# Plain projections for the first pair of width tiles of each SwiGLU, and another pairing of the features in the rest

## The chip, the cores and the metric

The kernel runs on one core of a Trainium2 chip. The metric is the time of one execution in microseconds (us): 1943.27 us, the median of three runs (1942.2 to 1945.07). The engines are named as the profile does: PE is TensorE, DVE is VectorE, ACT is ScalarE, POOL is GpSimd, SP is SyncE, which here only issues transfers. PEld is TensorE's loading of weights beside its matmuls.

## The reference, cut to what matters

A trunk of two layers works on one sequence of 512 tokens with 1024 features, in fp32:

```
D_MODEL = 1024; SEQ = 512; DEPTH = 2; D_FF = 2816
def rms_norm(x, g):
    y = x * rsqrt(mean(x * x, axis=-1, keepdims=True) + 1e-6)
    return y * g
def swiglu(x, w_gate, w_up, w_down):
    return (silu(x @ w_gate) * (x @ w_up)) @ w_down
for layer in range(2):
    x = x + 0.5 * swiglu(rms_norm(x, ffn_pre_norm[layer]), ...)
    x = x + mixer(rms_norm(x, mix_norm[layer]), ...)   # layer 0: even_mixer, layer 1: odd_mixer
    x = x + 0.5 * swiglu(rms_norm(x, ffn_post_norm[layer]), ...)
return rms_norm(x, final_norm)
```

There are four SwiGLUs. The even mixer stands between the first and the second, the odd one between the third and the fourth. The change leaves both mixers' own work as it is.

## The kernel before

x is kept transposed: eight tiles `x[0]` to `x[7]` of 128 features by 512 tokens. PE works on fp32 values split in two, a rounded high part and the rest, so each matrix product is three matmuls: high by high, high by low, low by high (`mm3`, L168 to L170). Weights come in chunks of 128x1024 (512 KB); ACT makes the high part `w_hi` (L120), then DVE the low part `w_lo` (L121).

**A SwiGLU** is `ffn(which, norm, feed)`, which = 0 to 3; the text calls them FFN0 to FFN3. Its width of 2816 is 22 tiles. `Step` s handles the tiles s and s+11 (HF = 11), for gate and up together. The two halves of the features, the two width tiles and the two halves of the tokens (`LO`, `HI`: 256 each) form a two by two block product, done with seven products in place of eight. Each product c is 24 matmuls of 256 columns (L406 to L408) into the banks A, B and D. Products take sums of weight chunks and sums of pieces of x. The seven sums of x are `xt[c, p]`, p = 0 to 3, with feature tile p paired with p+4; `SevenNorm.first`, `diff` and `rest` make them (L264 to L290) as soon as the tiles of x are final. The sums of weights are made by DVE in step 0 (L362) and by accumulating transfers of POOL's queue in the later steps (L351); plain weight loads are issued by SP (L349). The order of the products is `ORDER`, with product 1 of the next step inside. After the steps 3, 7 and 10 comes `down`, the projection back to x (`py`), which ends in DVE's update of `x[d]` (L485).

**The row factor.** RMSNorm's gain is put on x beforehand; its factor per token, `row`, is multiplied in after the products. For it every `x[d]` is squared (`square`: on POOL at L229, the last one on ACT at L227), the squares are added up on POOL (`acc`, L231), PE sums over the partitions (`pc`, L240), DVE makes the root (`rcol`, ten small instructions), PE spreads it (`pr`, L306) and ACT copies it (`R`, L310). `finish_soon(3)` puts `pc` three slots after the beginning of a SwiGLU and `pr` one slot later.

**The order of the work.** Each engine runs its own queue in order. `Stream.run` goes through slots, one product or projection each: first what was put off to this slot (`st.later(n, ...)`), then the splits of weights four items ahead (`split_to`), then loads, then the slot's matmuls. In the slots of a mixer's output projection (`out_proj`) the splits go only to the next slot. A scheduler then moves instructions within each engine's queue, so the queues quoted below are those after it. `feed(d)` is called as soon as `x[d]` is updated: from the last `down` of a SwiGLU (L485, before a mixer or before FFN2), or from `out_proj` (L526, before FFN1 and FFN3). For FFN0 the end of the program text (L1036 to L1071) does it by hand, on x as it arrives.

Of the kernel before, what the change touches and what calls it, by code (L numbers as in the profile page):

```python
# [18 lines left out]
P = 128  # L19
T = 512  # L20
# [12 lines left out]
def trunk_kernel(ctx: ExitStack, tc: tile.TileContext, a, out):  # L33
# [218 lines left out]
    LO, HI = slice(0, 256), slice(256, 512)  # L252

    class SevenNorm(Norm):


        def __init__(self, idx):
            super().__init__(idx)
            self.xt = {}

        def halves(self, c, p, src, g=None):
            t = t2k("r2", f"xt{c}", F32R).rearrange("p (n t) -> p n t", n=2)
            if g is None:
                nc.scalar.activation(t[:, 0], src, AF.Copy)  # L264
                nc.vector.tensor_sub(t[:, 1], src, t[:, 0].bitcast(F32))
            else:
                nc.scalar.activation(t[:, 0], src, AF.Copy, scale=g)
                nc.vector.scalar_tensor_tensor(t[:, 1], src, g, t[:, 0].bitcast(F32),  # L268
                                               op0=OP.mult, op1=OP.subtract)
            self.xt[c, p] = t  # L270

        def first(self, p):
            self.halves(1, p, x[p][:, LO], self.gain(p))

        def diff(self, p):
# [4 lines left out]
        def rest(self, p):  # L280
            q = p + 4
            g, n, nq = self.gain(q), neg_gains[:, self.idx, p:p + 1], neg_gains[:, self.idx, q:q + 1]
            ta, tb = tmp("x37"), tmp("x64")
            b22, x7, x6, x4 = ta[:, LO], ta[:, HI], tb[:, LO], tb[:, HI]
            nc.scalar.activation(b22, x[q][:, HI], AF.Copy, scale=g)
            nc.vector.scalar_tensor_tensor(x7, x[p][:, HI], n, b22, op0=OP.mult, op1=OP.add)
            nc.vector.scalar_tensor_tensor(x6, x[p][:, LO], n, x7, op0=OP.mult, op1=OP.subtract)
# [871 lines left out]
```

## Time and profile before

| what | us |
|---|---|
| median of three runs | 1943.27 |
| the profiled execution: its own time | 1942.9 |
| its span in the trace | 1941.2 |
| PE matmuls, busy | 1834.8 (95%) |
| DVE busy | 1413.3 (73%) |
| ACT busy | 882.4 (45%) |
| POOL busy | 365.3 (19%) |

The span is the time from the first to the last instruction; 1.7 us of the execution's own time lie outside it. A busy share is an average over the whole span: PE has stretches without a gap, hundreds of microseconds long, and a few in which it waits, and its clock is granted in two levels, 1.2 and 2.4 GHz, which the profile writes as shares of the higher one.

### The profile page before, as it was taken

How to read it: one execution, taken by the hardware profiler on the slowest of the kernel's cores; microseconds unless marked ns; L12 is line 12 of the kernel's file. 1: busy time of each engine (PE TensorE's matmuls, PEld its weight loads, DVE VectorE, ACT ScalarE, POOL GpSimd, SP SyncE). 2: the span in 40 equal slices, each digit the busy share in tenths (PEclk: the TensorE clock that was granted, in tenths of full speed). 3: DMA queues.
4: the chain of work that ended last, by engine and by line, in shares of the span. 5: the costliest groups of instructions: out<-in, count | busy, mean ns of one | idle time of the engine just before them, and what ended most of it. 6: DMA issues, size and time to landing. Idle time of an engine off the chain costs nothing.

```text
span 1941.2 us, 29617 instructions
## 1 busy us (share of the span) xinstructions
PE 1834.8 (95%) x11900; PEld 1681.6 (87%) x11900; DVE 1413.3 (73%) x1999; ACT 882.4 (45%) x1319; POOL 365.3 (19%) x310
## 2 busy tenths in 40 slices
PE   4999999989897999999789999999899969999997
PEld 4999989878776989989689898988788769899896
DVE  7866847766759856848987485687798798668474
ACT  5534525433644634525455253444555345345252
POOL 0000000542523000000310000034333230000003
PEclk7999999999997999999999999999999979999999
DMA  4755646412223655655256565542222226556461
GB/s 153 185 152 132 174 119 169 141 59 72 87 87 74 172 148 149 166 127 156 76 142 164 132 178 146 149 133 79 87 88 87 88 62 178 152 142 173 113 166 48
DMA packets 123897, 247.71 MB, mean 128 GB/s; under 512 B 9824, under 2 KB 19952, under 8 KB 123760
## 3 DMA queue, kind: packets, MB, share of 16 engines
q1 hardware_dynamic: 101392, 202.80, 33.2%
q0 software_dynamic: 21792, 41.98, 13.4%
q8 instruction: 93, 1.52, 0.3%
q10 hardware_dynamic: 576, 1.05, 0.1%
q14 instruction: 44, 0.36, 0.1%
HBM read 237.40 MB, written 2.10 MB: 123 GB/s over the span
## 4 chain that ended last, share of the span: by engine, by line
PE 80%; DVE 11%; POOL 4%; ACT 3%; issue 2%; DMA 1%; SPq 0%; DVEq 0%; POOLq 0%; ACTq 0%
PE pA L406 9%; PE py L168 9%; PE py L169 9%; PE pA L407 9%; PE pA L408 9%; PE py L170 8%; PE pD L408 4%; PE pD L407 4%; PE pD L406 4%; PE pB L406 2%; PE pB L407 2%; PE pB L408 2%; DVE w_lo L121 2%; DVE xt L268 1%; POOL q L592 1%
## 5 line engine op out<-in xcount | busy, mean ns | idle before, releaser
L120 ACT ACTIVATE w_hi<-w_raw 128x1024 fp32r<-128x1024 f32 (+1 forms) x455 | 473.7, 1043 | 614.8 <-PE py L169 228.1
L121 DVE TENSOR_TENSOR w_lo<-w_raw,w_hi 128x1024 fp32r<-128x1024 f32 (+1 forms) x455 | 565.1, 1242 | 183.5 <-ACT w_hi L120 151.2
L406 PE MATMUL pA<-xt,w_hi 128*128 128x256 f32 x1408 | 401.5, 285 | 26.1 <-ACT v L418 16.2
L407 PE MATMUL pA<-xt,w_hi 128*128 128x256 f32 x1408 | 400.2, 284 | 0.0
L408 PE MATMUL pA<-xt,w_lo 128*128 128x256 f32 x1408 | 399.9, 284 | 0.0
L351 POOL DMA_DIRECT2D w_raw<-in_gu x80 | 95.3, 1191 | 1075.0 <-DMA w_raw<-in_gu 658.6
L406 PEld LDWEIGHTS pA<-xt,w_hi 128*128 128x128 f32 x1408 | 272.4, 193 | 28.0 <-ACT v L418 18.0
L169 PE MATMUL py<-hl,w_hi 128*128 128x512 f32 x704 | 274.2, 390 | 0.0
L170 PE MATMUL py<-hh,w_lo 128*128 128x512 f32 x704 | 273.9, 389 | 0.0
L168 PE MATMUL py<-hh,w_hi 128*128 128x512 f32 x704 | 273.1, 390 | 0.0
L407 PEld LDWEIGHTS pA<-xt,w_hi 128*128 128x128 f32 x1408 | 272.3, 193 | 0.1
L408 PEld LDWEIGHTS pA<-xt,w_lo 128*128 128x128 f32 x1408 | 271.9, 193 | 0.2 <-DVE w_lo L1057 0.2
L406 PE MATMUL pD<-xt,w_hi 128*128 128x256 f32 x704 | 202.4, 287 | 15.9 <-ACT w_hi L120 15.9
L408 PE MATMUL pD<-xt,w_lo 128*128 128x256 f32 x704 | 202.6, 288 | 7.4 <-DVE w_lo L121 7.4
L407 PE MATMUL pD<-xt,w_hi 128*128 128x256 f32 x704 | 201.9, 287 | 0.0
L485 DVE SCALAR_TENSOR_TENSOR x<-py,x 128x512 f32<-128x512 f32 x96 | 65.9, 688 | 170.6 <-PE py L170 170.6
L168 PEld LDWEIGHTS py<-hh,w_hi 128*128 128x128 f32 x704 | 131.9, 188 | 28.1 <-ACT hh L459 1.2
L169 PEld LDWEIGHTS py<-hl,w_hi 128*128 128x128 f32 x704 | 132.2, 188 | 27.5 <-DVE hl L464 0.8
L170 PEld LDWEIGHTS py<-hh,w_lo 128*128 128x128 f32 x704 | 132.2, 188 | 27.3
L406 PEld LDWEIGHTS pD<-xt,w_hi 128*128 128x128 f32 x704 | 137.9, 196 | 16.8 <-ACT w_hi L120 16.5
L408 PEld LDWEIGHTS pD<-xt,w_lo 128*128 128x128 f32 x704 | 137.9, 196 | 8.0 <-DVE w_lo L121 8.0
L407 PEld LDWEIGHTS pD<-xt,w_hi 128*128 128x128 f32 x704 | 138.0, 196 | 0.3
(218 smaller groups left out, 3330.6 us busy)
## 6 DMA issues: line engine op xcount, KB each, us to landing
w_raw<-in_gu SPq DMA_DIRECT2D x215, 512.0 KB, 4.4
w_raw<-in_gu POOLq DMA_DIRECT2D x80, 512.0 KB, 7.2
w_raw<-in_wd SPq DMA_DIRECT2D x128, 256.0 KB, 2.9
w_raw<-in_wd SPq DMA_DIRECT2D x64, 192.0 KB, 2.5
w_raw<-in_oqk SPq DMA_DIRECT2D x16, 512.0 KB, 3.8
ks<-ks SPq DMA_DIRECT2D x24, 256.0 KB, 3.3
w_raw<-in_eqk SPq DMA_DIRECT2D x8, 512.0 KB, 3.6
w_raw<-in_eo SPq DMA_DIRECT2D x8, 512.0 KB, 4.0
```

What stands on the lines that cost most here:

```text
L120: nc.scalar.activation(hi, raw, AF.Copy)
L121: nc.vector.tensor_sub(lo, raw, hi.bitcast(F32))
L168: nc.tensor.matmul(o, sh, mh, start=first, stop=False)
L169: nc.tensor.matmul(o, sh, ml, start=False, stop=False)
L170: nc.tensor.matmul(o, sl, mh, start=False, stop=last)
L268: nc.vector.scalar_tensor_tensor(t[:, 1], src, g, t[:, 0].bitcast(F32), op0=OP.mult, op1=OP.subtract)
L351: nc.gpsimd.dma_start(t, src, accum_op=OP.add)
L406: nc.tensor.matmul(o, w[0][:, s], t[:, 0], start=new and p + g == 0, stop=False, **go)
L407: nc.tensor.matmul(o, w[0][:, s], t[:, 1], start=False, stop=False, **go)
L408: nc.tensor.matmul(o, w[1][:, s], t[:, 0], start=False, stop=p == 3, **go)
L485: nc.vector.scalar_tensor_tensor(x[d], py[d], 0.5, x[d], op0=OP.mult, op1=OP.add)
L592: nc.gpsimd.tensor_add(q, q, sw)
```

## The change

In every SwiGLU the pair (0, 11) is no longer a step of seven products. It is three slots of ordinary projections over all 512 tokens with x's own high and low parts: `first` (gate and up of tile 0 together, 48 matmuls of 512 columns), `gate` (tile 11, 24 matmuls) and `up` (tile 11, 24). `feed(k)` now splits the whole tile (`split`, L217 and L218), squares it on ACT and adds it on POOL (DVE in FFN0); the sums of x that steps 1 to 10 need are put off by a slot (`sums_for`) or to the end of `up` (`last_sums`). The products 1, 2 and 3 read halves of x's own parts (`whole`). Features are paired anew, with `KLO` and `KHI`; a half of the features is then every other pair of tiles in the chunk, and each weight load of a step, plain or accumulating, is two transfers of 256 KB with rows of 1 KB in place of one of 512 KB with rows of 2 KB. `finish_soon` counts from the first slot: 1 (2 in FFN0) in place of 3. The start of FFN0 is rewritten: x and the first two weight chunks arrive in three cuts, and `sums_for` comes two slots after.

```diff
+    KLO, KHI = (0, 1, 4, 5), (2, 3, 6, 7)
...
+        def halves(self, t, src):
+            nc.scalar.activation(t[:, 0], src, AF.Copy)
+            nc.vector.tensor_sub(t[:, 1], src, t[:, 0].bitcast(F32))
+
+        def whole(self, p):
+
+            k, q = KLO[p], KHI[p]
+            for c, i, s in ((1, k, LO), (2, q, LO), (3, q, HI)):
+                self.xt[c, p] = (self.hi[i][:, s], self.lo[i][:, s])
+
+        def sums_for(self, p):
+            k, q = KLO[p], KHI[p]
+            n, nq = neg_gains[:, self.idx, k:k + 1], neg_gains[:, self.idx, q:q + 1]
+            ta, tb = tmp("x17"), tmp("x26")
+            x1, x7, b22, x6 = ta[:, LO], ta[:, HI], tb[:, LO], tb[:, HI]
+            if p % 2 == 0:
+                self.x4 = tmp("x4")
+            x4 = self.x4[:, (LO, HI)[p % 2]]
+            new = {c: t2k("r2", f"xt{c}", F32R).rearrange("p (n t) -> p n t", n=2) for c in (5, 6, 7)}
+            nc.scalar.activation(b22, x[q][:, HI], AF.Copy, scale=self.gain(q))
+            nc.vector.tensor_sub(x1, x[k][:, HI], x[k][:, LO])
+            nc.vector.scalar_tensor_tensor(x7, x[k][:, HI], n, b22, op0=OP.mult, op1=OP.add)
+            nc.vector.scalar_tensor_tensor(x6, x[k][:, LO], n, x7, op0=OP.mult, op1=OP.subtract)
+            nc.scalar.activation(new[5][:, 0], x1, AF.Copy, scale=n)
+            self.halves(new[6], x6)
+            nc.vector.scalar_tensor_tensor(new[5][:, 1], x1, n, new[5][:, 0].bitcast(F32),
+                                           op0=OP.mult, op1=OP.subtract)
+            self.halves(new[7], x7)
             nc.vector.scalar_tensor_tensor(x4, x[q][:, LO], nq, x6, op0=OP.mult, op1=OP.subtract)
-            self.halves(7, p, x7)
-            self.halves(4, p, x4)
-            self.halves(3, p, b22)
+            for c, t in new.items():
+                self.xt[c, p] = (t[:, 0], t[:, 1])
+            self.rest[p] = x4
+
```

```diff
+        def last_sums(self):
+
+            for p in range(4):
+                k = KLO[p]
+                t = (self.hi[k][:, HI], self.lo[k][:, HI])
+                nc.scalar.activation(t[0], self.rest[p], AF.Copy)
+                nc.vector.tensor_sub(t[1], self.rest[p], t[0].bitcast(F32))
+                self.xt[4, p] = t
+
+        def square(self, k, by_act=False):
+            new = self.acc is None
+            if new:
+                self.acc = t2k("row", "acc")
+            sq = self.acc if new else tmp("sq")
+            nc.scalar.activation(sq, x[k], AF.Square)
+            if not new:
+                (nc.vector if by_act else nc.gpsimd).tensor_add(self.acc, self.acc, sq)
 
         def feed(self, k):
-            if k < 4:
-                self.first(k)
-                self.diff(k)
-            else:
-                self.rest(k - 4)
+            self.split(k)
             self.square(k)
+            if k in KHI:
+                st.later(1, lambda: self.sums_for(KHI.index(k)))
```

```diff
-                            nc.sync.dma_start(t, src)
-                        else:
-                            nc.gpsimd.dma_start(t, src, accum_op=OP.add)
+                        for g in range(2):
+                            src = gu[what[i], g].rearrange("p (a h c) -> p a h c", a=2, h=2)[:, :, what[i + 1]]
+                            dst = t[:, g].rearrange("p (a c) -> p a c", a=2)
+                            if i == 0:
+                                nc.sync.dma_start(dst, src)
+                            else:
+                                nc.gpsimd.dma_start(dst, src, accum_op=OP.add)
                 return go
...
+        def product(f, pg, pu):
+            t = act.tile([P, 2, T], F32, name="gu", tag="e", bufs=3)
+            g, u = t[:, 0], t[:, 1]
+            nc.vector.tensor_mul(g, pg, norm.row)
+            nc.scalar.activation(g, g, AF.Silu)
+            nc.vector.tensor_mul(u, pu, norm.row)
+            nc.vector.tensor_mul(u, u, g)
+            H[f] = split(u, "h", "h")
+
+        banks = {}
+
+        def first(wg, wu):
+            norm.finish_soon(1 + int(which == 0))
+            pg, pu = bank("pg"), bank("pu")
+            for ks in [[k] for k in range(KT)] if which == 0 else (range(KT - 1), range(KT - 1, KT)):
+                for b, w in ((pg, wg), (pu, wu)):
+                    project(b, w, norm, ks)
+            for p in range(4):
+                norm.whole(p)
+            st.later(2 + int(which == 0), lambda: product(0, pg, pu))
+
+        def gate(f):
+            def fn(w):
+                banks[f] = bank("pg")
+                project(banks[f], w, norm)
+            return fn
+
+        def up(f):
+            def fn(w):
+                b = bank("pu")
+                project(b, w, norm)
+                st.later(1, lambda: product(f, banks[f], b))
+                st.later(1, norm.last_sums)
+            return fn
+
+        st.add([chunk(gu[0, 0]), chunk(gu[0, 1])], first, dense=True, raws=6)
+        st.add([chunk(gu[HF, 0])], gate(HF), dense=True, raws=6)
+        st.add([chunk(gu[HF, 1])], up(HF), dense=True, raws=6)
+        add(1, 1)
         for s0, s1 in PARTS:
-            for s in range(s0, s1):
+            for s in range(max(s0, 1), s1):
                 for c in ORDER:
                     if c != 1:
                         add(s, c)
```

```diff
+    raws = [w4("w_raw").rearrange("p n t -> p (n t)") for _ in range(2)]
+    parts = [[w4(n, F32R).rearrange("p n t -> p (n t)") for n in ("w_hi", "w_lo")] for _ in range(2)]
+    cuts = [slice(0, 256), slice(256, 512), slice(512, 1024)]
     for q, s in enumerate(cuts):
-        nc.sync.dma_start(a11[:, :, s], gu0[:, :, s])
-        for k in ((0,), (1,), (2, 3))[q]:
-            load_x(k, LO)
-    st.tokens[0] = lambda: st.slots[0][2].tiles.update(a11=a11)
-    for k in range(4):
-        load_x(k, HI)
-    st.raws = 6
...
-    for k in range(4):
-        first.rest(k)
-        if k == 1:
-            st.split_to(3)
+        ks = ((0, 1), (2, 3), (4, 5, 6, 7))[q]
+        for c in range(2):
+            hi, lo = parts[c]
+            nc.scalar.activation(hi[:, s], raws[c][:, s], AF.Copy)
+            nc.vector.tensor_sub(lo[:, s], raws[c][:, s], hi[:, s].bitcast(F32))
+            for k in (ks[:1], ks[1:])[c]:
+                norms[0].split(k)
+    st.loaded = st.pres = 2
+    st.halves += parts
     for k in range(KT):
-        first.square(k, by_act=True)
+        norms[0].square(k, by_act=True)
+    for p in range(4):
+        st.later(2, lambda p=p: norms[0].sums_for(p))
     st.run()
 
```

The queue of DVE at the end of the even mixer's output projection, before FFN1. Before, `w_lo_5442` and `w_lo_5522` are the weights of that projection's last two slots, `w_lo_5554` those of FFN1's first product, `x3` to `x5` the tiles of x:

```order
L121 TENSOR_TENSOR w_lo_5442<-w_raw_5167,w_hi_5441 128x1024 [waits DMAHW6_49,DMAHW2_49]
L268 SCALAR_TENSOR_TENSOR xt5_5426<-x1_5424,gains_78,xt5_5426 128x256 [waits Activation_49]
L526 TENSOR_TENSOR x4_74<-py_5139,x4_74 128x512 [waits PE_49]
L526 TENSOR_TENSOR x5_75<-py_5152,x5_75 128x512 [waits PE_49]
L286 SCALAR_TENSOR_TENSOR x37_5458<-x0_70,neg_gains_80,x37_5458 128x256 [waits Activation_49]
L121 TENSOR_TENSOR w_lo_5522<-w_raw_5432,w_hi_5521 128x1024 [waits DMAHW7_49]
L287 SCALAR_TENSOR_TENSOR x64_5459<-x0_70,neg_gains_80,x37_5458 128x256 [waits DVE_49]
L121 TENSOR_TENSOR w_lo_5554<-w_raw_5434,w_hi_5553 128x1024 [waits DMAHW0_49,Activation_49]
```

And now, in the same place; `w_lo_5473` is the last slot's, `w_lo_5508` that of FFN1's first projection, and L282 to L264 are `sums_for(1)`:

```order
L264 TENSOR_TENSOR xt7_5401<-x17_5396,xt7_5401 128x256 [waits Activation_49]
L282 TENSOR_TENSOR x17_5413<-x1_71 128x256 [waits Pool_49]
L283 SCALAR_TENSOR_TENSOR x17_5413<-x1_71,neg_gains_80,x26_5414 128x256 [waits Activation_49]
L575 TENSOR_TENSOR x5_75<-py_5118,x5_75 128x512 [waits PE_49]
L284 SCALAR_TENSOR_TENSOR x26_5414<-x1_71,neg_gains_80,x17_5413 128x256 [waits DVE_49]
L287 SCALAR_TENSOR_TENSOR xt5_5415<-x17_5413,neg_gains_80,xt5_5415 128x256 [waits Activation_49]
L290 SCALAR_TENSOR_TENSOR x4_5398<-x3_73,neg_gains_80,x26_5414 128x256 [waits DVE_49]
L264 TENSOR_TENSOR xt6_5416<-x26_5414,xt6_5416 128x256 [waits Activation_49]
L264 TENSOR_TENSOR xt7_5417<-x17_5413,xt7_5417 128x256 [waits Activation_49]
L121 TENSOR_TENSOR w_lo_5473<-w_raw_5382,w_hi_5472 128x1024 [waits DMAHW7_49]
L218 SCALAR_TENSOR_TENSOR xl_5443<-x4_74,gains_78,xh_5442 128x512 [waits Activation_49]
L121 TENSOR_TENSOR w_lo_5508<-w_raw_5384,w_hi_5507 128x1024 [waits DMAHW0_49,PE_49,Activation_49]
```

The sums of x for two pairs (L282 to L264, one set of seven stands here, the other lies just before) are now ahead of the last slot's weights, where parts of `first` and `diff` and one instruction of `rest` were.

PE's queue near the beginning of FFN2. Before, the row sums `pc` stood between the product 5 (into D) and the product 2 (into B):

```order
L407 MATMUL pD_9220<-xt5_8977,w_hi_9082 128x256
L408 MATMUL pD_9220<-xt5_8977,w_lo_9083 128x256
L240 MATMUL pc_9273<-ones1_87,acc_8884 128x1 [waits Pool_49]
L240 MATMUL pc_9273<-ones1_87,acc_8884 128x1 x3
L406 MATMUL pB_9305<-xt2_9017,w_hi_9179 128x256 [waits Activation_49]
L407 MATMUL pB_9305<-xt2_9017,w_hi_9179 128x256
L408 MATMUL pB_9305<-xt2_9017,w_lo_9180 128x256 [waits DVE_49]
```

And now, between `first` (into `pg` and `pu`) and `gate`:

```order
L168 MATMUL pu_9113<-xh_9082,w_hi_9002 128x512
L169 MATMUL pu_9113<-xl_9083,w_hi_9002 128x512
L170 MATMUL pu_9113<-xh_9082,w_lo_9003 128x512
L240 MATMUL pc_9162<-ones1_87,acc_8810 128x1 [waits Pool_49]
L240 MATMUL pc_9162<-ones1_87,acc_8810 128x1 x3
L168 MATMUL pg_9196<-xh_8806,w_hi_9055 128x512
L169 MATMUL pg_9196<-xl_8807,w_hi_9055 128x512
L170 MATMUL pg_9196<-xh_8806,w_lo_9056 128x512
```

The row sums have moved from 48 matmuls of 256 columns behind the beginning of the SwiGLU to 48 of 512 columns, and the last matmuls ahead of them are those that read `x7`'s parts.

DVE's queue at the beginning of FFN0. Before, with the sums of weights (L362) and of x (L286, L287):

```order
L362 TENSOR_TENSOR w_sum_112<-w_raw_108,w_raw_110 128x1024 [waits DMAHW4_49,DMAHW3_49]
L362 TENSOR_TENSOR w_raw_108<-w_raw_108,w_raw_96 128x1024 [waits DVE_49]
L121 TENSOR_TENSOR w_lo_159<-w_sum_112,w_hi_158 128x1024 [waits Activation_49]
L286 SCALAR_TENSOR_TENSOR x37_162<-x0_70,neg_gains_80,x37_162 128x256
L362 TENSOR_TENSOR w_sum_112<-w_sum_112,w_raw_96 128x1024 [waits DVE_49]
L287 SCALAR_TENSOR_TENSOR x64_163<-x0_70,neg_gains_80,x37_162 128x256 [waits DVE_49]
```

And now; `acc` is the sum of squares, `w_lo_186` belongs to `gate`, `w_lo_192` to `up`, and L191 and L194 are the first of the ten small instructions of `rcol`:

```order
L218 SCALAR_TENSOR_TENSOR xl_157<-x7_77,gains_78,xh_156 128x512 [waits DMAHW5_49,Activation_49]
L311 TENSOR_TENSOR acc_160<-acc_160,sq_180 128x512 [waits DVE_49]
L121 TENSOR_TENSOR w_lo_186<-w_raw_183,w_hi_185 128x1024 [waits DMAHW6_49,Activation_49]
L282 TENSOR_TENSOR x17_267<-x0_70 128x256
L283 SCALAR_TENSOR_TENSOR x17_267<-x0_70,neg_gains_80,x26_268 128x256 [waits Activation_49]
L191 TENSOR_SCALAR rs0_378<-pc_372 128x4 [waits PE_49]
L284 SCALAR_TENSOR_TENSOR x26_268<-x0_70,neg_gains_80,x17_267 128x256 [waits DVE_49]
L287 SCALAR_TENSOR_TENSOR xt5_270<-x17_267,neg_gains_80,xt5_270 128x256 [waits Activation_49]
L290 SCALAR_TENSOR_TENSOR x4_269<-x2_72,neg_gains_80,x26_268 128x256 [waits DVE_49]
L264 TENSOR_TENSOR xt6_271<-x26_268,xt6_271 128x256 [waits Activation_49]
L264 TENSOR_TENSOR xt7_272<-x17_267,xt7_272 128x256 [waits Activation_49]
L282 TENSOR_TENSOR x17_284<-x1_71 128x256
```

The ten small instructions now stand among `sums_for`'s.

## Rows read from the trace of the kernel before

**Rows 1.** The page: busy us of the engines, share of the span, instructions.

```profile
PE 1834.8 (95%) x11900; PEld 1681.6 (87%) x11900; DVE 1413.3 (73%) x1999; ACT 882.4 (45%) x1319; POOL 365.3 (19%) x310
```

**Rows 2.** Windows: stretch, length, busy us (count) of PE, PEld, DVE, ACT, POOL; clock; DMA share; GB/s.

```profile
117.69:161.24 43.55, 43.55 (x194) 36.06 (x193) 20.75 (x23) 11.35 (x12) 3.58 (x3) 1.00 0.51 122
190.03:230.35 40.32, 40.32 (x338) 40.32 (x337) 34.23 (x38) 22.81 (x28) 3.57 (x3) 1.00 0.66 171
```

**Rows 3.** Windows: the starts of the SwiGLUs, to the end of step 0's third product.

```profile
0.00:57.21 57.21, 30.00 (x204) 29.23 (x205) 44.94 (x88) 32.70 (x61) 5.14 (x12) 0.82 0.54 157
569.61:635.08 65.47, 49.42 (x290) 44.69 (x289) 58.94 (x86) 30.71 (x53) 21.88 (x16) 0.84 0.32 81
953.97:996.59 42.62, 27.16 (x206) 26.55 (x205) 37.02 (x63) 21.47 (x39) 11.22 (x8) 0.84 0.38 99
1541.60:1607.93 66.33, 49.12 (x289) 44.29 (x287) 59.69 (x87) 30.63 (x53) 22.65 (x17) 0.82 0.30 80
```

**Rows 4.** Waits of PE: line waited for, total us, times, longest us.

```profile
PE pA L406 <- ACT v L418: 16.2, 2, 15.4
PE pD L406 <- ACT w_hi L120: 15.9, 3, 7.4
PE py L170 <- DVE w_lo L121: 15.3, 2, 8.2
PE pc L240 <- POOL acc L231: 11.3, 1, 11.3
```

**Rows 5.** Timeline of PE: matmuls at the start of FFN1 (start us, duration, operation).

```profile
585.89 0.80 PE L170 MATMUL py<-mh,w_lo 128*128 128x512 f32 x1 [7.07 <-DVE w_lo L121]
...
589.47 0.63 PE L169 MATMUL py<-m,w_hi 128*128 128x512 f32 x1
```

**Rows 6.** Timeline of DVE at the start of FFN1.

```profile
572.03 1.29 DVE L526 TENSOR_TENSOR x<-py,x 128x512 f32<-128x512 f32 x2 [0.82 <-PE py L170]
573.30 0.82 DVE L268 SCALAR_TENSOR_TENSOR xt<-x,gains,xt 128x256 fp32r<-128x256 f32 x1
574.05 2.70 DVE L277 TENSOR_TENSOR x<-x 128x256 f32<-128x256 f32 x2
...
581.63 0.48 DVE L268 SCALAR_TENSOR_TENSOR xt<-x,gains,xt 128x256 fp32r<-128x256 f32 x1
...
593.85 0.41 DVE L265 TENSOR_TENSOR xt<-x,xt 128x256 fp32r<-128x256 f32 x1
```

**Rows 7.** Timeline of POOL in the same place, and at the start of FFN2.

```profile
572.81 1.04 POOL L229 TENSOR_TENSOR acc<-x 128x512 f32<-128x512 f32 x1 [10.81 <-DVE x L526]
573.81 1.22 POOL L229 TENSOR_TENSOR sq<-x 128x512 f32<-128x512 f32 x1
575.11 1.36 POOL L231 TENSOR_TENSOR acc<-acc,sq 128x512 f32<-128x512 f32 x1
...
971.80 2.98 POOL L231 TENSOR_TENSOR acc<-acc,sq 128x512 f32<-128x512 f32 x1 [4.66 <-ACT sq L227]
```

**Rows 8.** DMA issues: KB each, median us from issue to landing.

```profile
w_raw<-in_gu SPq DMA_DIRECT2D x215, 512.0 KB, 4.4
w_raw<-in_gu POOLq DMA_DIRECT2D x80, 512.0 KB, 7.2
w_raw<-in_wd SPq DMA_DIRECT2D x128, 256.0 KB, 2.9
```

**Rows 9.** Timeline: one accumulating load, the split that reads it, and the product after.

```profile
191.48 1.19 POOL L351 DMA_DIRECT2D w_raw<-in_gu  x1 [9.47 <-DVE gu L435]
...
201.68 1.06 ACT L120 ACTIVATE w_hi<-w_raw 128x1024 fp32r<-128x1024 f32 x1 [1.02 <-PE pD L407]
...
210.19 0.28 PE L406 MATMUL pA<-xt,w_hi 128*128 128x256 f32 x1
```

**Rows 10.** Timeline of ACT and DVE at FFN0's beginning.

```profile
14.03 0.51 ACT L285 ACTIVATE x<-x,gains 128x256 f32<-128x256 f32 x1 [2.31 <-DMA x<-in_xT]
...
15.82 1.22 DVE L121 TENSOR_TENSOR w_lo<-w_sum,w_hi 128x1024 fp32r<-128x1024 f32 x1
```

More of the change, by code (lines that the diff above doesn't have):

```diff
@@ L295, in feed @@
-        def feed(self, k):
-            if k < 4:
-                self.first(k)
-                self.diff(k)
-            else:
-                self.rest(k - 4)
+            self.xt, self.rest = {}, {}
+        def halves(self, t, src):
[5 more added lines that the diff above has]
+                self.xt[c, p] = (self.hi[i][:, s], self.lo[i][:, s])
@@ L346, in go @@
                     for i in range(0, len(what), 2):
-                        src = gu[what[i]].rearrange("g p c -> p g c")[:, :, what[i + 1] * T:(what[i + 1] + 1) * T]
-                        if i == 0:
-                            nc.sync.dma_start(t, src)
-                        else:
-                            nc.gpsimd.dma_start(t, src, accum_op=OP.add)
+                        for g in range(2):
[5 more added lines that the diff above has]
+                                nc.gpsimd.dma_start(dst, src, accum_op=OP.add)
                 return go
@@ L365, in new @@
                     r["z"] = w4("w_sum")
-                if self.s > 0:
+                if True:
                     by_sum = {
@@ L405, in fn @@
                             s = slice((g * 4 + p) * P, (g * 4 + p + 1) * P)
-                            nc.tensor.matmul(o, w[0][:, s], t[:, 0], start=new and p + g == 0, stop=False, **go)
-                            nc.tensor.matmul(o, w[0][:, s], t[:, 1], start=False, stop=False, **go)
-                            nc.tensor.matmul(o, w[1][:, s], t[:, 0], start=False, stop=p == 3, **go)
+                            nc.tensor.matmul(o, w[0][:, s], t[0], start=new and p + g == 0, stop=False, **go)
+                            nc.tensor.matmul(o, w[0][:, s], t[1], start=False, stop=False, **go)
+                            nc.tensor.matmul(o, w[1][:, s], t[0], start=False, stop=p == 3, **go)
                     for n, aux in enumerate(after):
@@ L493, in add @@
             st.add([steps[s].item(c)], steps[s].slot(c), dense=True, raws=6)
-        add(0, 1)
-        first, end, fn, dense, raws = st.slots[-1]
-        def begin(w):
-            norm.finish_soon(3)
-            fn(w)
-        begin.tiles = steps[0].raw
-        st.slots[-1] = (first, end, begin, dense, raws)
+        def product(f, pg, pu):
[32 more added lines that the diff above has]
+        add(1, 1)
         for s0, s1 in PARTS:
-            for s in range(s0, s1):
+            for s in range(max(s0, 1), s1):
                 for c in ORDER:
@@ L1033, in trunk_kernel @@
     ffn(3, norms[5], last_feed)
[L1036 to L1068 removed]
+    raws = [w4("w_raw").rearrange("p n t -> p (n t)") for _ in range(2)]
+    parts = [[w4(n, F32R).rearrange("p n t -> p (n t)") for n in ("w_hi", "w_lo")] for _ in range(2)]
+    cuts = [slice(0, 256), slice(256, 512), slice(512, 1024)]
+    for q, s in enumerate(cuts):
+        for c in range(2):
+            nc.sync.dma_start(raws[c][:, s], a["gu0"][0, c][:, s])
+            if q == 0:
+                nc.sync.dma_start(x[c], a["xT"][c])
+        for k in ((), (2, 3), (4, 5, 6, 7))[q]:
+            nc.sync.dma_start(x[k], a["xT"][k])
+    for q, s in enumerate(cuts):
+        ks = ((0, 1), (2, 3), (4, 5, 6, 7))[q]
+        for c in range(2):
+            hi, lo = parts[c]
[5 more added lines that the diff above has]
+    st.halves += parts
     for k in range(KT):
[L1070 removed]
+        norms[0].square(k, by_act=True)
+    for p in range(4):
+        st.later(2, lambda p=p: norms[0].sums_for(p))
     st.run()
```

45 lines of the change are left out of this document (removed).

## The prediction

> **What bounds the kernel now.** I read the page first: PE is busy for 95% of the span [rows 1], so only two things can move the time much, PE's own work and the few places where it stands. Then the windows over a stretch without gaps. A projection runs 192 matmuls of 512 columns in 43.55 us, 0.227 each; two steps of seven products run 336 matmuls of 256 columns in 40.32 us, 0.120 each, so a product takes 2.88 us and a step 20.16 [rows 2]. In both PE is busy throughout at the full clock, and DVE has time left. Third, the same view over the four starts, each up to the end of the third product of step 0, which is where step 1's product 5 begins: 57.21, 65.47, 42.62 and 66.33 us long, with PE idle for 27.2, 16.1, 15.5 and 17.2, together 76, and a clock of 0.82 to 0.84 [rows 3]. The list of waits names what ends last there: the x sums and weight sums that the first products need (one `pA` wait of 15.4, `pD` waits up to 7.4), the weights of the output projection (8.2), the sum of squares (11.3) [rows 4]. The steady part is bound by PE alone; the starts are bound by DVE's queue and what it shares with POOL.
>
> **Work of PE.** Up to the mark there are eight products before, 192 x 0.120 = 23.0 us. Now there are 96 matmuls of 512 columns and product 1 of step 1: 96 x 0.227 + 2.9 = 24.7. That is 1.6 us more per SwiGLU, 6.5 in all, and it is contained in the four sums below.
>
> **FFN0.** Before, the mark is at 57.21 [rows 3]. x4 was in by 14.03, behind 2.75 MB with it [rows 10]; all of x and two weight chunks are 3 MB, so x7 is in by about 15 and its parts are ready at 16.5. The low part of `gate`'s weights follows on DVE at about 18, which is also when `first` ends. From there PE has 5.4 + 0.8 + 5.4 of work, to about 30. The row factor decides: its ten small instructions stand among `sums_for`'s. DVE has four sets of sums, each seven operations of 0.41 to 0.48 us that overlap by 0.07, 2.6 a set [rows 6], so 10.5; three weight splits of 1.22, overlapping likewise, 3.4 [rows 10]; leftover additions of squares and the ten small ones, some 3; and waits for ACT, some 1.5. That is 36.4. Then `pr`, 0.4, and product 1, 2.9 at the full and 5.8 at the half clock: about 42.5, a gain of 14.7. Bounds: if the scheduler's order keeps the factor off the lane, PE's own work ends about 36 at the low clock (gain 21); if every sum waits for ACT, about 48 (gain 9).
>
> **FFN1 and FFN3.** What PE needs next is `w_lo_5473`, now queued behind two sets of sums. From 572.03 [rows 6] DVE has six updates of x at 0.64, 3.9; four low parts of x at about 0.70 (between 0.48 for 256 columns and 1.22 for 1024, [rows 6, 10]), 2.8; `w_lo_5393`, 1.1; two sets of sums, 5.2; its own 1.1. Together 14.1, so 586.1 undisturbed. POOL holds DVE up: between 573.30 and 576.75 three operations that take 0.48 + 0.41 + 0.41 alone took 0.82 + 2.70 [rows 6], 2.2 more, while POOL was at work for nearly all of that time [rows 7]; the updates, which read PSUM, kept their 0.64. Weighted by the kind of operation I take 0.6 of POOL's time. Five additions of 1.36 fall there: 4.1. The low part is done at 590.2, PE goes on at 590.5. It was ready for it at about 584: before, it ended its earlier matmuls 7.07 us before 585.89 [rows 5], and the chunk that it waited for then is now split early, so it has 22 matmuls more first. So 6.5 us of waiting; before, matmuls behind such a wait were 0.63 long at an interval of 0.43 instead of 0.227 for ten of them, from 585.89 past 589.47 [rows 5], so 2.0 for the clock. Then 20 matmuls of the projection, 4.5; the ordinary pair, 21.8; `pc` and `pr`, 1.2; product 1, 2.9. The mark falls at 590.5 + 2.0 + 4.5 + 21.8 + 1.2 + 2.9 = 622.9 instead of 635.08, a gain of 12.2. FFN3 has the same queues and nearly the same window: 12.2 again. What hides the rest: `first` reads x7's parts only in its last six matmuls, 9.5 us behind its beginning, and the sums of squares are wanted 10.9 behind it. Bounds: undisturbed (no loss beside POOL) the gain is 16.3, without a clock loss 18.9; with the sums of the next pairs in front of the following weights too, 5.
>
> **FFN2.** PE comes from the last `down` without a gap and has 953.97 as its beginning [rows 3]. Before, it stood 11.3 us for the last addition of squares [rows 4], done at 974.78 [rows 7], and at 0.8 and 3.4 for others. Now POOL has seven additions instead of seven products and seven additions, and DVE no weight sums. The last update of x can be made at 954; square, two additions and a split later is about 959, and `pc` is due at 953.97 + 10.9 = 964.9: covered by six microseconds. The mark: 953.97 + 10.9 + 0.8 + 5.4 + 0.4 + 5.4 + 2.9 = 979.8, and 1 us for the row factor's ten small steps, which `gate`'s 5.4 only just covers: 980.8 instead of 996.59, a gain of 15.8. Bounds 12 to 16.8.
>
> **The steady part.** The products of steps 1 to 10 are the same matmuls. Their loads are doubled in number. SP issues ten instead of five per step; POOL four instead of two, 1.19 each [rows 9], 4.8 us in a step of 20.16, so neither queue is full. The later half of an accumulating load is issued 1.2 later. Its cover: issued at 191.48, landed 7.2 later [rows 8], the split begins at 201.68 and PE needs it at 210.19 [rows 9]; with 1.06 and 1.22 for the two splits some 9 us of delay cost nothing, 8 with what else stands in those queues. Nearest rows: 256 KB loads take 2.9 where 512 KB take 4.4 [rows 8], so two in a row 1.3 times as long; twice as long would be 14.4, a delay of 7.2. Both are under the cover. I take 0 for the 40 steps, with 0 to 10 as bounds; no gain, since nothing is waited for there.
>
> **The sum.** 14.7 + 12.2 + 15.8 + 12.2 = 54.9. The profiled execution took 1942.9 us, 1.7 beside its span: 1888.0. The median of the three runs is 0.4 above it, so 1888.4; I say 1888.
>
> **The rivals.**
> Lost again at the starts: DVE becomes the bound of every start, since splits of x, sums and weight splits are on one lane. For it: DVE is busy for 58.9 of 65.5 us there already [rows 3], and its queue has the sums ahead of weights. Against it: the weight sums (four of 1.22) go, and so do four low parts per pair. Priced by the lower bounds, 9 + 6 + 12 + 6 = 33 are gained: 1910.
> Held for the whole: DVE loses the full time of each addition on POOL. For it: where DVE's operations read SBUF alone, it lost 2.2 us beside about 3 of POOL's [rows 6, 7], more than the 0.6 that I take as the mean. Against it: the updates of x between them lost nothing. 5 x 1.36 = 6.8 instead of 4.1 in FFN1 and FFN3, 2.7 later at each: 1893. The Trainium skill, "SBUF — State Buffer", section "Who interferes with whom", says this of a DVE instruction with two SBUF inputs and a GpSimd instruction that reads SBUF: one excludes the other for the whole instruction. By that rule the time would be that of this rival; the rows agree in kind, and lie between it and the forecast in size.
> More than forecast: POOL and DVE get out of each other's way, because half of POOL's work went to ACT, and the row factor of FFN0 is not held up. For it: ACT is busy less than half of each start [rows 3]. Against it: the additions on POOL remain. 18 + 17.5 + 16.8 + 17.5 = 70: 1873.
> Slower than before: the smaller transfers with 1 KB rows fall behind. Place: the accumulating loads of steps 1 to 10. It decides from a landing more than 15.5 us after the issue, against 7.2 now: each microsecond beyond is lost 40 times, and from 1.4 us per step the gain is eaten. At 2 per step, 80 - 55 = 25 worse: 1968. For it: the DMA engines are busy for 0.66 of a steady stretch [rows 2], and the loads come in turn. Against it: the landing would have to double and more. The Trainium skill, "DMA: Bandwidth & Descriptors", section "Rules for kernel authors", asks to coalesce transfers into large ones, which speaks for this rival; no row here shows accumulating loads of the smaller form.
> The starts stay as they are: the waits are only renamed, with another lane as slow. Against it: the 11.3 us for the squares and the 15.4 of FFN0 have known causes in work that goes. 1943.
>
> **How the numbers follow.** Forecast 50%, held for the whole 13%, more than forecast 15%, lost again at the starts 15%, transfers 5%, no difference 2%. The time is the likeliest's, 1888. The range takes the forecast with the bounds of its four terms (about 1877 to 1903), the greater gain down to 1868, and the case of 1910 with 12 us beyond, to 1922; what lies outside are the transfers, the unchanged start and the tails. A measurement of this kernel can tell 0.2%, some 4 us, from no change. Faster 0.93, same 0.02, slower 0.05.
>
> **What would show it.** Marks at about 42.5, 608, 954 and 1553 (the later ones shifted by the gains before them); `pc` of FFN2 without a wait; one wait of about 6 us of PE for a low part of weights in each output projection before FFN1 and FFN3; a wait of some 7 us for the row factor in FFN0; 40.32 us for two steps as before; accumulating loads that land in 8 to 14 us. Wrong would be: gaps of PE inside steps 1 to 10, waits for `w_hi` behind a DMA there, a wait for `acc` in FFN2, or a start that is no shorter.

## The result, and the profile after

The changed kernel takes 1889.67 us, the median of four runs (1887.48 to 1890.68), against 1943.24 of the kernel before beside it: a ratio of 0.9722, with a 95% interval of 0.9705 to 0.9739. Run a second time beside the last experiments it took 1887.32 (0.9703, 0.9689 to 0.9718), so a difference of 2 to 3 us between two kernels below is not told from none. 1888 was predicted, in a range of 1868 to 1922.

The first row of the page, as in [rows 1]: PE is busy for the same 1835 us; what went is idle time, 52 us of the span.

```profile
PE 1834.6 (97%) x11612; PEld 1663.2 (88%) x11612; DVE 1359.1 (72%) x1949; ACT 875.4 (46%) x1302; POOL 415.0 (22%) x369
```

The windows, columns as in [rows 2]: the four starts up to step 1's product 5, which answer to [rows 3], and two steps of seven products, which answer to the second of [rows 2].

```profile
0.00:43.53 43.53, 31.56 (x133) 25.73 (x133) 36.70 (x79) 28.21 (x52) 8.71 (x15) 0.88 0.80 218
555.75:610.12 54.37, 49.01 (x219) 39.91 (x218) 46.36 (x77) 32.09 (x53) 17.39 (x13) 0.91 0.42 97
928.98:955.17 26.19, 26.19 (x133) 22.09 (x132) 24.63 (x45) 13.61 (x24) 7.04 (x6) 1.00 0.49 114
1500.64:1555.78 55.14, 48.51 (x217) 39.09 (x215) 47.11 (x78) 32.02 (x53) 17.49 (x13) 0.94 0.41 96
176.57:216.89 40.32, 40.32 (x339) 40.32 (x338) 34.24 (x38) 22.82 (x28) 6.49 (x6) 1.00 0.70 175
```

The halves of the accumulating loads, which answer to the second row of [rows 8]:

```profile
w_raw<-in_gu POOLq DMA_DIRECT2D x160, 256.0 KB, 5.3
```

The starts are shorter by 13.7, 11.1, 16.4 and 11.2 us, 52.4 together, which is the whole difference of the spans (1941.2 and 1888.9). PE's idle time in them fell from 76 to 24 us. Its busy time in them stayed (155.3 against 155.7), though the prediction reckons with 6.5 us more work: less of it ran at the low clock (a clock of 0.88 to 1.00 instead of 0.82 to 0.84). FFN2's start has no gap any more and runs at the full clock. The steady steps take the same 40.32. PE's waits, as in [rows 4]:

```profile
PE pg L168 <- ACT w_hi L120: 10.0, 2, 5.1
...
PE pr L322 <- DVE rcol L202: 6.3, 1, 6.3
PE pg L168 <- ACT xh L217: 5.5, 1, 5.5
...
PE py L170 <- DVE w_lo L121: 2.0, 3, 0.8
```

The waits of [rows 4] for sums and for `acc` are gone. What is left at the starts are one wait of some 5 us in each output projection with short ones for low parts of weights behind it, FFN0's wait for the row factor, and its first 5.5 us, until the first high part of x is made. The matmuls at FFN1's beginning (start, duration, operation, wait before it), as in [rows 5]:

```profile
575.52 0.80 PE L168 MATMUL pg<-xh,w_hi 128*128 128x512 f32 x1 [4.86 <-ACT w_hi L120]
576.82 0.79 PE L170 MATMUL py<-mh,w_lo 128*128 128x512 f32 x1 [0.50 <-DVE w_lo L121]
```

And DVE's queue there, as in [rows 6], then POOL's, as in [rows 7]:

```profile
558.17 1.89 DVE L575 TENSOR_TENSOR x<-py,x 128x512 f32<-128x512 f32 x3 [0.82 <-PE py L170]
...
562.04 2.33 DVE L121 TENSOR_TENSOR w_lo<-w_raw,w_hi 128x1024 fp32r<-128x1024 f32 x1
564.29 1.78 DVE L218 SCALAR_TENSOR_TENSOR xl<-x,gains,xh 128x512 fp32r<-128x512 f32 x1
565.99 1.51 DVE L282 TENSOR_TENSOR x<-x 128x256 f32<-128x256 f32 x1
...
571.67 0.68 DVE L575 TENSOR_TENSOR x<-py,x 128x512 f32<-128x512 f32 x1
572.27 0.89 DVE L284 SCALAR_TENSOR_TENSOR x<-x,neg_gains,x 128x256 f32<-128x256 f32 x1
573.08 0.47 DVE L287 SCALAR_TENSOR_TENSOR xt<-x,neg_gains,xt 128x256 fp32r<-128x256 f32 x1
573.48 1.48 DVE L290 SCALAR_TENSOR_TENSOR x<-x,neg_gains,x 128x256 f32<-128x256 f32 x1
...
575.55 1.21 DVE L121 TENSOR_TENSOR w_lo<-w_raw,w_hi 128x1024 fp32r<-128x1024 f32 x1
```

```profile
561.81 5.41 POOL L311 TENSOR_TENSOR acc<-acc,sq 128x512 f32<-128x512 f32 x3 [13.93 <-ACT sq L309]
571.38 1.50 POOL L311 TENSOR_TENSOR acc<-acc,sq 128x512 f32<-128x512 f32 x1 [4.15 <-ACT sq L309]
573.21 1.47 POOL L311 TENSOR_TENSOR acc<-acc,sq 128x512 f32<-128x512 f32 x1 [0.34 <-ACT sq L309]
...
583.62 1.29 POOL L311 TENSOR_TENSOR acc<-acc,sq 128x512 f32<-128x512 f32 x1 [6.83 <-ACT sq L309]
```

The three operations that meet the first three additions are each 1.0 to 1.1 us longer than alone (1.21, 0.74, 0.41); those additions take 1.8 each, where one that met none of them, at 583.62, takes 1.29. The update at 571.67, which reads PSUM, runs beside an addition at its usual 0.68.

### The profile page after: what moved, and what is told of

It is laid out like the page before. It is cut to its first block, busy times and chain, and to the rows that moved or that the text cites. A ratio compares the mean times of both kernels' runs of the same rounds, so it can differ in the third digit from the quotient of the medians.

```text
span 1888.9 us, 29622 instructions
## 1 busy us (share of the span) xinstructions
PE 1834.6 (97%) x11612; PEld 1663.2 (88%) x11612; DVE 1359.1 (72%) x1949; ACT 875.4 (46%) x1302; POOL 415.0 (22%) x369
## 3 DMA queue, kind: packets, MB, share of 16 engines
q0 software_dynamic: 43552, 41.98, 15.1%
## 4 chain that ended last, share of the span: by engine, by line
PE 82%; DVE 7%; POOL 4%; ACT 3%; issue 2%; DMA 1%; SPq 0%; DVEq 0%; POOLq 0%; ACTq 0%
PE py L168 10%; PE py L170 10%; PE py L169 9%; PE pA L424 8%; PE pA L425 8%; PE pA L426 8%; PE pD L426 4%; PE pD L425 4%; PE pD L424 4%; PE pB L426 2%; PE pB L425 2%; PE pB L424 2%; POOL q L641 1%; DVE w_lo L121 1%; ACT e L690 1%
## 5 line engine op out<-in xcount | busy, mean ns | idle before, releaser
L424 PE MATMUL pA<-xh,w_hi 128*128 128x256 f32 x640 | 182.7, 285 | 0.0
L425 PE MATMUL pA<-xl,w_hi 128*128 128x256 f32 x640 | 182.1, 285 | 0.0
L426 PE MATMUL pA<-xh,w_lo 128*128 128x256 f32 x640 | 182.1, 285 | 0.0
L424 PE MATMUL pA<-xt,w_hi 128*128 128x256 f32 x640 | 181.2, 283 | 0.0
L426 PE MATMUL pA<-xt,w_lo 128*128 128x256 f32 x640 | 181.1, 283 | 0.0
L425 PE MATMUL pA<-xt,w_hi 128*128 128x256 f32 x640 | 181.1, 283 | 0.0
L424 PEld LDWEIGHTS pA<-xh,w_hi 128*128 128x128 f32 x640 | 123.9, 194 | 1.5 <-ACT v L436 1.4
L425 PEld LDWEIGHTS pA<-xl,w_hi 128*128 128x128 f32 x640 | 123.9, 194 | 0.1
L426 PEld LDWEIGHTS pA<-xh,w_lo 128*128 128x128 f32 x640 | 123.9, 194 | 0.0
L424 PEld LDWEIGHTS pA<-xt,w_hi 128*128 128x128 f32 x640 | 122.9, 192 | 0.2 <-ACT v L436 0.2
L426 PEld LDWEIGHTS pA<-xt,w_lo 128*128 128x128 f32 x640 | 122.9, 192 | 0.0
L425 PEld LDWEIGHTS pA<-xt,w_hi 128*128 128x128 f32 x640 | 122.9, 192 | 0.0
```

The lines of the kernel that those rows point to most:

```text
L424: nc.tensor.matmul(o, w[0][:, s], t[0], start=new and p + g == 0, stop=False, **go)
L425: nc.tensor.matmul(o, w[0][:, s], t[1], start=False, stop=False, **go)
L426: nc.tensor.matmul(o, w[1][:, s], t[0], start=False, stop=p == 3, **go)
```

## The experiments

Times are medians; "the changed kernel" is 1887 to 1890. Edits are against the changed kernel where nothing else is said. The ratios are to the kernel before, which took 1944.4, 1943.8 and 1945.4 beside the three groups of experiments. "Marks" below are the beginnings of step 1's product 2 in a SwiGLU (in the kernel before, of step 0's), and a stretch goes from one mark to the next.

**Squares on POOL again.**

```diff
-            nc.scalar.activation(sq, x[k], AF.Square)
+            if by_act or k == KT - 1:
+                nc.scalar.activation(sq, x[k], AF.Square)
+            else:
+                nc.gpsimd.tensor_mul(sq, x[k], x[k])
```

> The changed kernel with the squares of x's tiles 0 to 6 made on POOL again (the change's other parts stay). Theory (DVE's queue, held up beside POOL, sets the starts): in each of FFN1 and FFN3 five multiplies of some 1.2 us come to stand beside DVE's sums, of which DVE loses 0.65, so the low part of the last slot's weights comes 3.9 us later in each; FFN2 hides it or loses up to 3. 8 to 11 us slower than the changed kernel, 1898 to 1901. Rival (the squares on ScalarE are where most of the gain comes from): over 25 us slower, above 1915. Second rival (POOL does not hold up DVE): 1890.

Measured 1906.48, 0.9802 (0.9788 to 0.9817): 17 to 19 slower, between the theory's range and the rival's. FFN1 and FFN3 lost 3 to 5 each by their marks, as the theory had it. Nearly half of the loss lies where the theory allowed 0 to 3, in FFN2. Its window, 26.19 long in the changed kernel, and the waits of PE:

```profile
930.99:966.00 35.01, 30.55 (x133) 24.31 (x133) 32.00 (x51) 16.14 (x27) 11.76 (x9) 0.90 0.42 94
```

```profile
PE pg L168 <- ACT w_hi L120: 15.7, 2, 8.0
...
PE pg L169 <- DVE xl L218: 3.2, 2, 2.2
```

The first row of waits belongs to the output projections (10.0 in the changed kernel), the second to FFN2. There PE is idle for 4.5 us, 3.2 of it for x's low parts, which stand on DVE between operations held up, and part of the window runs at the low clock (0.90). So the squares' place does matter where DVE is just able to keep up.

**The kernel before with its squares on ACT** (against before; 0, 2, 3 and 5 are the four SwiGLUs' norms).

```diff
-            if by_act or k == KT - 1:
+            if by_act or k == KT - 1 or self.idx in (0, 2, 3, 5):
```

> The kernel before with all squares of the four SwiGLUs made on ACT, and nothing else of the change. Putting them back on POOL cost the changed kernel 17 us. Theory (the squares hold DVE's queue up in either kernel, by what stands there): FFN1 and FFN3 gain 3 to 5 each, FFN2's wait of 11.3 for the sum of squares shrinks by 3 to 8: 1924 to 1935. Rival (the squares matter only where the sums of x are delayed as in the changed kernel): 1939 to 1945. Second rival (they were the main cost of the starts): below 1915.

1923.91, 0.9894 (0.988 to 0.9909): 20 faster than before, at the theory's better end. FFN1, FFN2 and FFN3 gained 6 to 6.5 each by their marks, for FFN1 and FFN3 more than the theory's 3 to 5. PE's waits for the low parts of the output projection's weights fell from the 15.3 of [rows 4] to 3.8: with the squares off POOL, DVE makes those parts sooner. The sum of squares is still waited for, though for 8.5 instead of 11.3, and the long waits for sums are untouched:

```profile
PE pA L406 <- ACT v L418: 16.2, 2, 15.4
PE pD L406 <- ACT w_hi L120: 16.1, 3, 8.2
...
PE pc L240 <- POOL acc L231: 8.5, 1, 8.5
...
PE py L170 <- DVE w_lo L121: 3.8, 2, 2.4
```

So the squares are worth 17 to 20 of the 54 us by either kernel. The other 34 to 37 are a difference and no run has them alone: they hold the ordinary pair, the new pairing and FFN0's rewritten start, whose window alone is 13.7 shorter.

**Sums of x at once.**

```diff
-                st.later(1, lambda: self.sums_for(KHI.index(k)))
+                self.sums_for(KHI.index(k))
```

> The changed kernel with the sums of x of FFN1, FFN2 and FFN3 made as soon as the tiles are final, and not a slot later, so only the ordinary first pair, the pairing and the squares on ACT are left of the change there. Theory (what the ordinary pair gives is time: nothing of the sums is needed until 22 us after its beginning, so their exact place matters only where weights or x's parts wait behind them): FFN2 0 to 2 slower, FFN1 and FFN3 2 to 6 slower each, 1892 to 1904. Rival (the delay by a slot is what pays): over 1910.

1890.9, 0.9723 (0.9709 to 0.9738): the same as the changed kernel, just under the theory's range. The delay by one slot is worth nothing that can be measured. By elimination, what pays is that nothing needs the sums for the length of the ordinary pair; no run tests that alone.

**Half loads in the kernel before.**

```diff
-                        if i == 0:
-                            nc.sync.dma_start(t, src)
-                        else:
-                            nc.gpsimd.dma_start(t, src, accum_op=OP.add)
+                        for q in range(2):
+                            cut = slice(q * 256, (q + 1) * 256)
+                            if i == 0:
+                                nc.sync.dma_start(t[:, :, cut], src[:, :, cut])
+                            else:
+                                nc.gpsimd.dma_start(t[:, :, cut], src[:, :, cut], accum_op=OP.add)
```

> The kernel before, with each weight load of its steps as two transfers of 256 KB with rows of 1 KB, plain and accumulating, and nothing else of the change. Theory (nothing waits for these loads in the steps, and they have 8 us in hand): no difference, 1941 to 1946. Rival (smaller transfers cost time that the change then had to make up for): 2 us per step or more, above 1990; or, if halves land sooner, faster at the starts, by up to 5.

1945.36, 1.0006 (0.9996 to 1.0016): no difference. Two steps still take 40.32 us, and the accumulating halves land in a median of 5.7 us after their issue, where whole loads took 7.2 [rows 8]:

```profile
191.59:231.91 40.32, 40.32 (x339) 40.32 (x338) 34.24 (x38) 22.84 (x28) 7.25 (x6) 1.00 0.70 171
```

```profile
w_raw<-in_gu POOLq DMA_DIRECT2D x160, 256.0 KB, 5.7
```

**Additions of squares on DVE in FFN1 and FFN3.**

```diff
-            self.square(k)
+            self.square(k, by_act=self.idx in (2, 5))
```

> The changed kernel with the additions of squares of FFN1 and FFN3 on DVE instead of POOL. Theory (POOL's additions hold DVE up: in the changed kernel DVE's operations in front of the last slot's weights took 4.4 us more than the same operations alone): with none of them DVE does the five additions in 3.0 and nothing is held, so the weights come 1.4 earlier in each, 1886 to 1889. Rival (the longer operations have another cause, such as ACT's or a DMA's use of the same memory): DVE's operations stay as long, and the additions come on top, 3 us later in each, 1895 to 1898.

1883.74, 0.9683 (0.9667 to 0.9699): 4 to 6 faster by the medians, more than the theory said, though the interval overlaps that of the changed kernel's second run. By the marks FFN3's stretch is 3.6 shorter and FFN1's 1 to 3. The rival is out by the trace: with no addition on POOL there, the operations that took 2.33, 1.78 and 1.51 in the changed kernel take what they take alone, beside the same squares on ACT:

```profile
563.29 0.74 DVE L218 SCALAR_TENSOR_TENSOR xl<-x,gains,xh 128x512 fp32r<-128x512 f32 x1
...
564.55 1.21 DVE L121 TENSOR_TENSOR w_lo<-w_raw,w_hi 128x1024 fp32r<-128x1024 f32 x1
565.69 0.41 DVE L282 TENSOR_TENSOR x<-x 128x256 f32<-128x256 f32 x1
```

**The row factor first in FFN0.**

```diff
-            norm.finish_soon(1 + int(which == 0))
+            norm.finish_soon(1)
...
-        st.later(2, lambda p=p: norms[0].sums_for(p))
+        st.later(3, lambda p=p: norms[0].sums_for(p))
```

> The changed kernel, with FFN0's sums of x put off by one more slot and its row factor asked for one slot earlier, so that the ten small instructions stand at the head of DVE's queue behind the split of gate's weights. Theory (DVE's order sets FFN0's beginning: PE waited 6.3 us for the row factor and then ran product 1 at half the clock, 2.6 more): the wait for the factor falls to 2 at most, and then the weights' low part for product 1 is late, by about 4; the mark at 43.5 moves to 38 to 40, 1884 to 1887. Rival (the lane is full whatever its order): 43.5 stays, 1890.

1886.71, 0.9701 (0.9687 to 0.9716). The trace shows the theory's order of things: the wait of 6.3 for the factor is gone, product 1 waits 1.2 and product 5 0.75 for weights,

```profile
32.69 0.39 PE L424 MATMUL pA<-xh,w_hi 128*128 128x256 f32 x1 [1.21 <-ACT w_hi L120]
33.94 0.39 PE L424 MATMUL pD<-xt,w_hi 128*128 128x256 f32 x1 [0.75 <-ACT w_hi L120]
```

and product 2 of step 1 begins at 43.9 instead of 49.5 (48.2 in the changed kernel's second run). Not all of that is kept: at 45.8 PE waits 1.46 for the high part of the next product's weights, a wait that the changed kernel does not have there. The time alone, 1 to 3 us better than the changed kernel's two medians, does not tell it from no change.

**Sums behind the projection's weights in FFN1 and FFN3.**

```diff
-            if k in KHI:
+            if k in KHI and self.idx == 3:
                 st.later(1, lambda: self.sums_for(KHI.index(k)))
...
             for p in range(4):
                 norm.whole(p)
+            if which in (1, 3):
+                for p in range(4):
+                    st.later(1, lambda p=p: norm.sums_for(p))
```

> The changed kernel with all sums of x in FFN1 and FFN3 put off until the first slot of the ordinary pair has begun, so that they stand behind the weights of the output projection in DVE's and ACT's queues. Theory (PE's two waits in each output projection, 5.4 and 6.6 us together, and the half clock after them, some 3, come from the sums that stand in front of weights; the ordinary pair has room for 10.5 us of sums): both waits go, 8 us in each, 1872 to 1876. Rival (the sums are then late for product 5 of step 1, and the time is only moved): 1886 to 1892.

1886.04, 0.9695 (0.968 to 0.9709): at the better edge of the rival's range. In FFN1 the wait for weights fell, from 5.4 to 2.1, and did not go as the theory had it; 2.7 came back as a wait for the row factor, whose ten instructions now stood behind the sums:

```profile
571.73 0.66 PE L170 MATMUL py<-mh,w_lo 128*128 128x512 f32 x1 [2.09 <-DVE w_lo L121]
...
598.54 0.65 PE L322 MATMUL pr<-ident,rcol 128*128 128x128 f32 x4 [2.65 <-DVE rcol L202]
```

FFN1's stretch is as long as in the changed kernel. FFN3's is 3.4 shorter; there the wait for the factor is 1.2. So the rival holds for FFN1 and only in part for FFN3.

**Both, with the sums one slot later still** (`st.later(2, ...)` in the last edit, and the edit for FFN0).

> The changed kernel with FFN0's order as in the run with the row factor first, and with the sums of x in FFN1 and FFN3 behind the projection's weights and behind the row factor's instructions. Theory (the run with the sums late took away most of PE's wait for weights, but put the sums in front of the row factor, which gave 4 us back in FFN1 and 2 to 3 in FFN3): FFN0 gains 5, FFN1 3 to 6, FFN3 4 to 7 against the changed kernel: 1873 to 1880. Rival (DVE is full between the last update of x and product 5, so a wait comes up at product 1 or 5 in place of the factor's): 1881 to 1886.

1880.57, 0.967 (0.9655 to 0.9685), at the border of the two ranges. FFN0 and FFN3 gained 5 and 4 by their marks, FFN1's stretch nothing: there the scheduler filled DVE with three sets of sums before the factor, which PE then awaited for 3.9.

**Row factor first, additions on DVE** (the two edits together).

> The changed kernel with the row factor first in FFN0 and the additions of squares of FFN1 and FFN3 on DVE. Theory (the two gains lie in different starts and add up: 5.4 in FFN0, 2.8 and 3.6 in FFN1 and FFN3 by the marks of the two single runs): 11 to 12 us faster than the changed kernel, 1877 to 1880 by the medians. Rival (what one gains at a start is taken back in the next): 1883 or more.

1881.3, 0.967 (0.9654 to 0.9686), 6.0 better than the changed kernel beside it: neither range. FFN1's stretch, from FFN0's mark to its own, took 566.8 us here and 563.5 in the run with the additions alone. Of the 3.3 us between them, 1.5 is the wait that the row factor's new place brings right behind FFN0's mark. It stands in all four runs with the factor first and in none of the others:

```profile
46.07 0.39 PE L424 MATMUL pA<-xt,w_hi 128*128 128x256 f32 x1 [1.46 <-ACT w_hi L120]
```

So the rival is right for that part: of what FFN0 gains by its mark, 1.5 is given back in the next product. The other 1.8 is no more than what the two runs of the changed kernel differ by in the same stretch (566.4 and 564.7), and its cause is open.

**All three, the last two sets of sums later still** (`st.later(2 if p < 2 else 3, ...)`).

> As the run before, and the sums of x in FFN1 and FFN3 put behind the weights of the projection, the last two sets behind the row factor's instructions. Theory: with nothing held up and no sums in front of weights, PE waits at most 2 us in each output projection; the row factor is at most 2 us late: 3 to 6 better in FFN1 and FFN3 each than with the additions on DVE alone: 1868 to 1874. Rival (DVE is full in the ordinary pair, and the row factor or product 5 waits as long as the weights did): 1877 to 1881.

1875.84, 0.9645 (0.963 to 0.9659), between the ranges: the fastest, 11.5 us better than the changed kernel beside it (1887.32) and 69.6 better than before. The starts of FFN1, FFN2 and FFN3 are 48.1, 26.2 and 49.0 long instead of 54.4, 26.2 and 55.1 in the changed kernel's first run, all at the full clock; PE still waits 1.3 and 2.6 us for low parts of weights in the output projections:

```profile
551.06:599.15 48.09, 45.83 (x219) 37.71 (x218) 44.57 (x84) 31.04 (x52) 6.51 (x6) 1.00 0.47 110
917.98:944.16 26.18, 26.18 (x133) 22.09 (x132) 24.56 (x45) 13.61 (x25) 7.04 (x6) 1.00 0.49 113
1489.78:1538.73 48.95, 45.35 (x216) 37.14 (x214) 45.31 (x85) 30.96 (x52) 6.53 (x6) 1.00 0.47 108
```

**The changed kernel beside these.**

> The changed kernel itself, on the same chip as the two runs beside it, as their measure: 1887 to 1892 by every theory.

1887.32, as given above.

## Why the prediction was right

- *Work of PE and the steady part.* Two steps take 40.32 before and after, and the half loads alone changed nothing. Cost 0, as taken. A half lands 5.3 to 5.7 after its issue, a whole load took 7.2; with the second half issued 1.2 later that is below the 1.3 times that I had taken from the plain loads. The landing in 8 to 14 us, named as a sign of the forecast, did not occur; the loads were early, not late.
- *FFN2, forecast 15.8, measured 16.4.* `pc` waits for nothing; PE runs without a gap. The microsecond that I set aside for the row factor was not needed. But the cover was thinner than my six microseconds: POOL's last addition ended at 936.3, and `pc` came at 939.9:

```profile
932.83 3.44 POOL L311 TENSOR_TENSOR acc<-acc,sq 128x512 f32<-128x512 f32 x2
```

```profile
939.86 0.95 PE L240 MATMUL pc<-ones,acc 128*128 128x1 f32 x8
```

  The run with the squares back on POOL shows that FFN2 was close to a bound that I had priced at 0 to 3: there it lost 8.8.
- *FFN1 and FFN3, forecast 12.2 each, measured 11.1 and 11.2.* Counted from the first update of x, the low part of the last slot's weights was forecast at 18.2 us and came at 18.6 (558.17 to 576.76). DVE had just the items of that sum in between: six updates, four low parts of x, two sets of sums and two weight splits. The loss beside POOL, taken as 4.1, was 4.7 (1.1, 1.0, 1.1, 0.4 and 1.0 over the five operations that were lengthened). Two details were not foreseen. Most of the wait, 4.86, is put down to ACT's `w_hi` of FFN1's first projection: ACT makes the high parts of the sums and so stands behind DVE, and the scheduler had put one matmul of `first` ahead of the projection's. DVE's low part came 1.3 us behind that and ended the last wait, 0.50, as the forecast has it. And the clock cost 2.9 instead of 2.0: from the first of the 20 matmuls after the wait to the matmul behind them went 7.5 us instead of 4.5.
- *FFN0, forecast 14.7, measured 13.7.* The row factor was ready at 37.4 (36.4 forecast) for the reason given, its ten instructions among the sums; product 1 ran the whole way at the low clock, 5.3 us (5.8 forecast). That the sum came within 1 us is in part luck. The low part of `gate`'s weights was done at 19.6 and not at 18. Behind it DVE had no additions of squares left and waited 0.3 instead of 1.5, but it also did a sum of weights (L380) and four low parts of the last sums (L301), 2.5 together, which the forecast does not have:

```profile
17.81 0.68 DVE L311 TENSOR_TENSOR acc<-acc,sq 128x512 f32<-128x512 f32 x1
18.41 1.22 DVE L121 TENSOR_TENSOR w_lo<-w_raw,w_hi 128x1024 fp32r<-128x1024 f32 x1
...
27.22 0.42 DVE L301 TENSOR_TENSOR xl<-x,xh 128x256 fp32r<-128x256 f32 x1
...
35.69 1.22 DVE L380 TENSOR_TENSOR w_raw<-w_raw 128x1024 f32<-128x1024 f32 x1
...
37.22 0.16 DVE L202 SCALAR_TENSOR_TENSOR rcol<-rs,rs 128x4 f32<-128x4 f32 x1
```

- *Held for the whole.* DVE lost 4.7 us to five additions of 1.3 alone, 0.7 of their time, so neither the rival's whole nor nothing. With the additions on DVE, and the squares on ACT as they were, no operation was lengthened, so POOL's additions are the cause; that is now shown. "SBUF — State Buffer", section "Who interferes with whom", in the Trainium skill says that a VectorE instruction with two inputs in SBUF and a GpSimd instruction that reads SBUF exclude each other. The three hits of 1.0 to 1.1 agree with it in kind. The sum stays below the rival's price because no hit was as long as an addition, and one was much shorter: the addition at 571.38 ran beside an update of x, which reads PSUM, and cost 0.4.
- *What I did not price.* I treated the change by starts and not by parts. By parts the runs give 17 to 20 for the squares, 0 for the delay of the sums and 0 for the loads; the ordinary pair, the pairing and FFN0's new start share the other 34 to 37, and how is open. That the squares' place alone would cost FFN2 8.8 us stood nowhere in the prediction.
- *Slips in the sums.* In FFN1 the bound without any loss is 12.2 + 4.1 + 2.0 = 18.3, not 18.9. "Lost again" takes 6 where FFN1's lower bound is 5, so 31 are gained and the time is 1912, not 1910. The four terms' bounds added up give about 1867 to 1912, not 1877 to 1903. None of them moves the forecast; the range given holds all but 1 us of it.

The other rivals did not occur: transfers by the half-load run, lost again and unchanged starts by the windows. That more was to be had was right in kind: the row factor's place and POOL's additions, which I named as its two conditions, together with the sums' place gave 11.5 us more by the medians.

## What to carry to other kernels

Where an engine is bound in a steady part and starved at the seams, price each seam by the lane that is last there, in the order of its queue, and count the operations of that lane in front of the one that is awaited; four such sums came within 1.1 us of the trace each, one of them in part by luck, so look at the items too. A chain of small dependent instructions can be spread among bulk work by a scheduler while an engine waits for its end (16.7 us from the first to the last of ten in FFN0, with PE waiting 6.3): put it ahead of the bulk that is needed later, and look at what the bulk then delays (1.5 here). And an operation moved off a busy lane can still hold that lane: an addition on POOL cost DVE 0.9 us on average, where doing it on DVE itself took 0.6.

## What the runs showed of the hardware that was not expected

Accumulating transfers of half the size with rows of half the length landed sooner, 5.3 to 5.7 us against 7.2, though POOL's queue moved twice as many packets (43552 against 21792) for the same bytes. After the same wait of 6.3 us in FFN0, the two profiled runs of the changed kernel came to product 2 of step 1 at 49.5 and 48.2, with a different stretch at the lower clock (0.88 and 0.92 over the first 43.5 us); from there to the same product in FFN1 they took 566.4 and 564.7. Four runs of the changed kernel spread over 3.2 us, so differences of 2 to 3 us between two kernels are not read as theirs.
